# Softmax normalisation on ScalarE, head by head, in place of one VectorE product over four heads

## Chip, cores and metric

The kernel runs on one core of one Trainium2 chip. The metric is device time in microseconds; the kernel before takes 1180.76 us, the median of three runs (1177.13 to 1182.51). Engines are called by their names in the profile too: TensorE is PE (PEld its weight loads), VectorE DVE, ScalarE ACT, GpSimd POOL, and SyncE, which only issues DMAs here, SP.

## What is computed

One inference step of a two-layer decoder. Each layer normalises x (1024 prompt tokens and 8 sample tokens, 1024 channels), projects it through one matrix to pooling, attention and RWKV-7 inputs with their gates, and projects the concatenated results back. The change touches the attention, a sliding window of 128 with a learned sink per head:

```python
def _sink_softmax(s, mask, sinks):
    s = jnp.where(mask, s, -jnp.inf)
    sink = sinks.astype(jnp.float32)[:, :, None, None]
    m = jnp.maximum(jnp.max(s, axis=-1, keepdims=True), sink)
    p = jnp.exp(s - m)
    denom = jnp.sum(p, axis=-1, keepdims=True) + jnp.exp(sink - m)
    return p / denom

# per block of 128 queries:
p = _sink_softmax(s, mask, sinks.reshape(N_KV, Q_PER_KV))
o = jnp.einsum('bnkgqs,bnskd->bnqkgd', p.astype(vx.dtype), vx)
```

All values are float32. There are 8 heads of 64 channels, 2 key heads.

## The kernel before

**Stages.** The tokens are worked in two halves (H = 0: 512 prompt tokens and the 8 samples; H = 1: 512). Line 1542 and after give the order: input projection of layer 0 half 0, of half 1, output projection of half 0, then layer 1 half 0, output of layer 0 half 1, layer 1 half 1, and the two output projections of layer 1. Each projection multiplies high and low parts of weights and activations (three products per 128 channels, `acc<-hh,wh`, `acc<-hl,wh`, `acc<-hh,wl`, line 310). These products are "the projection products" below. The weights come by DMA, ScalarE casts their high part (`wh`) and GpSimd or VectorE makes the low part (`wl`).

**Streams beside the projections.** Attention, RWKV and the ends of the projection tiles are generators that run as jobs beside the projections (lines 270 to 352). Between two projection products `tick` lets every job go on whose due time has come. A due time is worked out by a planner: `Engine` (lines 120 to 152) books each VectorE, ScalarE and GpSimd instruction on that engine's account with a fixed part and a part per column (ScalarE 0.11 us and 0.00082 us a column, VectorE 0.07 and 0.00104, lines 162 to 164), and `after` (line 320) adds a margin to the time at which an operand should be there. TensorE's order is fixed by this planner; the order on the other engines is chosen by the framework's scheduler. Where a result is needed before anything else can go on, `need` (line 345) runs the jobs without projection products between them.

**Attention.** A block (`attn_block`, line 1135) is 128 queries of four heads: 2 layers times 2 halves times 4 query blocks times 2 groups of heads, 32 in all, and one sample job per layer (`attn_sample`). Its score products are `ps`. ScalarE and VectorE bring the current and the previous window into one tile `sm` of 128 queries by four heads by 129 columns, the sink in the last. `softmax` (line 1114) takes the minimum (the signs are turned), ScalarE's four exponentials with their sums, VectorE's reciprocal of the sums, and the product. Then `attn_values` (line 1173) transposes each head (`pt`), makes `pcur` (VectorE) and `pall` (ScalarE), and multiplies by the values (`po`). Three `sm` tiles exist, so a block's scores wait until the block three before is done; one block at a time may be between `pt` and `po` (`hold`, line 283). `open_attn` (line 1394) lets the next half's keys be finished only when all attention of the half before is done.

**RWKV.** Its scan goes in steps of 32 tokens, each with three small TensorE groups into `CA` and `CB`: from `XS,AG`, from `ys,TZ`, and from `XS,BT`, with short VectorE and ScalarE copies between. After eight steps come a group norm (`osb`, `gsm`) and the transposes back (`back`), then products on GpSimd. The last such group has to be done before line 1517, since the last products need it.

Of the kernel before, what the change touches and what calls it, by code (L numbers as in the profile page):

```python
# [12 lines left out]
AF = mybir.ActivationFunctionType  # L13
ALU = mybir.AluOpType
# [72 lines left out]
def hybrid_step_kernel(ctx: ExitStack, tc: tile.TileContext, I, O):  # L87
# [74 lines left out]
    V = Engine(nc.vector, 0.07, 0.00104)  # L162
# [93 lines left out]
    def tt(eng, out, a, b, op):  # L256
        eng.tensor_tensor(out=out, in0=a, in1=b, op=op)

    def act(out, in_, f, **kw):
        S.activation(out=out, in_=in_, func=f, **kw)  # L260
# [853 lines left out]
    def softmax(s, rows, nh):  # L1114

        sm = sb.tile([128, 2, 4], F32, tag="asm", name="asm", bufs=2)
        nm, su = (sm[:rows, i, :nh] for i in range(2))
        V.tensor_reduce(out=nm, in_=s, axis=AX.X, op=ALU.min)
        for i in range(nh):
            act(s[:, i, :], s[:, i, :], AF.Exp, scale=-1.0, bias=nm[:, i:i + 1], accum_out=su[:, i:i + 1])  # L1120
        V.reciprocal(out=su, in_=su)
        tt(V, s[:, :, 0:128], s[:, :, 0:128], su.unsqueeze(2).to_broadcast([rows, nh, 128]), ALU.mult)


    scored = []
# [9 lines left out]
    def attn_block(L, q, att, i, jp, mixed, after):  # L1135
# [25 lines left out]
        for e in range(2):  # L1161
# [4 lines left out]
            )  # L1166
        s4 = sm.rearrange("p e j k -> p (e j) k")
        softmax(s4, 128, 4)
        job = spawn(at_s[1], attn_values(L, att, i, jp, s4, done), (sm,))
        attn_jobs.append(job)  # L1170
# [34 lines left out]
    def attn_sample(L, q, att):  # L1205
# [30 lines left out]
        S.copy(out=s[:64, :128], in_=ps[:64, :128])  # L1236
        G.tensor_copy(out=s[:64, 128:129], in_=L.vd[:64, 17:18])
        softmax(s[:64].unsqueeze(1), 64, 1)
        yield (s,)
        yield from vacant("att")  # L1240
# [474 lines left out]
```

## Time and profile before

| | us |
|---|---|
| median of three runs | 1180.76 |
| the profiled execution, device time | 1182.06 |
| its span, first to last instruction | 1180.3 |
| PE busy | 1087.3 (92%) |
| DVE busy | 827.0 (70%) |
| ACT busy | 619.5 (52%) |
| POOL busy | 354.6 (30%) |
| mean granted TensorE clock | 0.958 of full |

How to read it: a busy TensorE is not TensorE at its peak, since matmuls are pipelined and their ends are modelled. Idle time of an engine that is not the bottleneck costs nothing. A group with one line (L150, L310) is recorded by a helper, so groups are told apart by the tile names; `sm<-sm,asm` is the softmax, `asm` the minimum and the sums.

### The profile page before, as it was taken

To read this page: it belongs to the slowest core of one execution; us is meant where nothing else is said; L and a number is where in the kernel's file an instruction comes from. 1 tells how busy PE (TensorE), PEld (TensorE's weight loads), DVE (VectorE), ACT (ScalarE), POOL (GpSimd) and SP (SyncE) were. 2 spreads that over 40 slices of the span, in tenths; PEclk is the share of its full clock that TensorE was granted. 3 is DMA by queue.
4 is the path that set the end of the run, shared out by engine and by line. 5 is a ranking of instruction groups with operands and counts; after the bars stand their busy time and mean duration, and the time that the engine had idled before them with its cause. 6 is when DMAs were issued, how large, how long until landed. Compare 5 with 4: busy or idle time off the path is not lost.

```text
span 1180.3 us, 24735 instructions
## 1 busy us (share of the span) xinstructions
PE 1087.3 (92%) x9258; PEld 872.2 (74%) x9258; DVE 827.0 (70%) x1783; ACT 619.5 (52%) x1579; POOL 354.6 (30%) x420
## 2 busy tenths in 40 slices
PE   6989897899899998989999979899999999899995
PEld 5989886576577677868988868666677677678864
DVE  6545889658867968577766988676855788877423
ACT  4435454557456663666446553475546566645331
POOL 5156535400131134430344534211112112333100
PEclk7999999999899998999999999899999999899997
DMA  6765344653255245644654335644575343454652
GB/s 194 225 195 167 120 142 152 201 182 102 77 170 153 75 143 170 211 152 138 197 166 126 111 106 152 223 139 157 194 227 171 119 153 107 132 184 145 184 155 93
DMA packets 116947, 183.27 MB, mean 155 GB/s; under 512 B 24398, under 2 KB 36190, under 8 KB 116828
## 3 DMA queue, kind: packets, MB, share of 16 engines
q1 hardware_dynamic: 116828, 181.70, 49.0%
q8 instruction: 72, 1.18, 0.4%
q14 instruction: 47, 0.39, 0.1%
HBM read 125.73 MB, written 50.62 MB: 149 GB/s over the span
## 4 chain that ended last, share of the span: by engine, by line
PE 61%; DVE 23%; DMA 4%; ACT 4%; issue 4%; POOL 2%; SPq 1%; POOLq 0%; DVEq 0%; ACTq 0%
PE acc L310 43%; PE CA L310 5%; DVE pr L150 3%; PE ps L310 2%; PE po L310 2%; PE CB L310 2%; DVE hl L150 2%; DMA sq<-z 2%; DVE sm L150 2%; DVE AG L150 1%; SPq L160 1%; DVE X L150 1%; PE pt L313 1%; DVE pd L150 1%; DVE z L150 1%
## 5 line engine op out<-in xcount | busy, mean ns | idle before, releaser
L310 PE MATMUL acc<-hh,wh 128*128 128x512 f32 (+2 forms) x1464 | 494.7, 338 | 17.9 <-ACT hh L150 9.4
L310 PE MATMUL acc<-hl,wh 128*128 128x256 f32 (+3 forms) x1464 | 493.8, 338 | 13.5 <-DVE hl L150 13.2
L310 PE MATMUL acc<-hh,wl 128*128 128x512 f32 (+2 forms) x1464 | 494.2, 339 | 8.7 <-POOL wl L150 5.7
L310 PEld LDWEIGHTS acc<-hh,wh 128*128 128x128 f32 x1464 | 284.8, 195 | 54.2 <-ACT hh L150 11.1
L310 PEld LDWEIGHTS acc<-hl,wh 128*128 128x128 f32 (+1 forms) x1464 | 282.9, 193 | 47.9 <-DVE hl L150 19.5
L310 PEld LDWEIGHTS acc<-hh,wl 128*128 128x128 f32 x1464 | 284.7, 195 | 45.2 <-issue 11.7
L150 ACT CAST wh<-wst 128x512 fp32r<-128x512 f32 (+1 forms) x246 | 148.8, 607 | 159.8 <-PE acc L310 109.8
L150 POOL TENSOR_TENSOR wl<-wst,wh 128x512 fp32r<-128x512 f32 x99 | 137.0, 1390 | 141.4 <-ACT wh L150 112.6
L150 DVE TENSOR_TENSOR pr<-X,N 128x4 f32<-128x4 f32 (+15 forms) x128 | 63.9, 499 | 6.8 <-POOL ro L150 3.2
L150 ACT ACTIVATE sm<-sm,asm 128x129 f32<-128x129 f32 x130 | 50.8, 393 | 17.5 <-DVE asm L150 17.3
L150 ACT ACTIVATE e<-e 128x520 f32<-128x520 f32 (+1 forms) x64 | 40.5, 633 | 26.7 <-DVE e L150 26.3
L150 POOL TENSOR_TENSOR z<-z,rope 128x520 f32<-128x520 f32 (+1 forms) x20 | 32.2, 1612 | 72.3 <-DMA sq<-z 59.9
L150 DVE TENSOR_REDUCE X<-pr 128x2 f32<-128x4 f32 (+15 forms) x128 | 44.8, 350 | 2.3
L150 POOL TENSOR_TENSOR mx<-mx,e 128x520 f32<-128x520 f32 (+1 forms) x24 | 33.2, 1381 | 42.5 <-ACT e L150 36.9
L150 ACT COPY XS<-CB 32x128 f32<-32x128 f32 (+2 forms) x88 | 27.3, 311 | 34.9 <-PE CB L310 34.2
L150 POOL TENSOR_TENSOR on<-on,bv 128x256 f32<-128x256 f32 x16 | 12.1, 779 | 110.5 <-ACT on L150 91.2
L150 ACT ACTIVATE XS<-CB,pc 64x64 f32<-64x64 f32 x112 | 28.7, 304 | 29.5 <-PE CB L310 28.4
L310 PE MATMUL ps<-kh,q 64*128 64x256 f32 (+1 forms) x256 | 39.0, 397 | 4.6 <-DVE sm L150 3.5
L150 POOL COPY sm<-vd 128x4 f32<-128x4 f32 (+1 forms) x34 | 8.2, 244 | 111.1 <-PE pt L313 81.8
L150 POOL COPY zs<-ev 128x9 f32<-128x9 f32 (+3 forms) x28 | 8.3, 298 | 107.1 <-DVE ev L150 90.2
L150 DVE COPY XS<-CA 32x128 f32<-32x128 f32 (+1 forms) x72 | 20.7, 288 | 26.8 <-PE CB L310 25.2
L150 DVE SCALAR_TENSOR_TENSOR hl<-xh,vec,hh 128x520 fp32r<-128x520 f32 (+1 forms) x32 | 28.0, 887 | 15.5 <-ACT hh L150 15.3
(250 smaller groups left out, 1925.5 us busy)
## 6 DMA issues: line engine op xcount, KB each, us to landing
wst<-in_w_in_dram SPq DMA_DIRECT2D x175, 256.0 KB, 3.1
kin<-wl SPq DMA_DIRECT2D x88, 256.0 KB, 3.4
wl<-kin SPq DMA_DIRECT2D x88, 256.0 KB, 2.7
wst<-in_w_out_dram SPq DMA_DIRECT2D x56, 256.0 KB, 3.5
kout<-wl SPq DMA_DIRECT2D x32, 256.0 KB, 3.5
zr<-mz SPq DMA_DIRECT2D x24, 256.0 KB, 3.2
xrkv<-zr SPq DMA_DIRECT2D x16, 384.0 KB, 4.1
wl<-kout SPq DMA_DIRECT2D x24, 256.0 KB, 3.1
```

Of the source, the lines that this page charges most:

```text
L150: return f(*a, **kw)
L160: return nc.sync.dma_start(out, in_)
L310: placed(T.matmul(out=out, lhsT=lhsT, rhs=rhs, start=start, stop=stop, **kw), n, out)
L313: placed(T.transpose(out=out, in_=in_, identity=identity), 300 if out.shape[0] > 64 else 130, out)
```

## The change

In `softmax` the one VectorE product of `sm` (128 queries by four heads by 128 columns) with the reciprocal sums, spread over the columns, is replaced by a loop over the heads: ScalarE copies each head's 128 columns in place, with the reciprocal sum of the row as a scale.

```diff
@@ -1119,7 +1119,8 @@
         for i in range(nh):
             act(s[:, i, :], s[:, i, :], AF.Exp, scale=-1.0, bias=nm[:, i:i + 1], accum_out=su[:, i:i + 1])
         V.reciprocal(out=su, in_=su)
-        tt(V, s[:, :, 0:128], s[:, :, 0:128], su.unsqueeze(2).to_broadcast([rows, nh, 128]), ALU.mult)
+        for i in range(nh):
+            act(s[:, i, 0:128], s[:, i, 0:128], AF.Copy, scale=su[:, i:i + 1])
 
 
     scored = []
```

The planner books the copies on ScalarE's account, so due times and with them the order of jobs shift. Three places follow; the orders before are given first.

ScalarE, layer 0 half 0, at the first three softmaxes (`sm,asm<-sm,asm` are the exponentials, `e`, `sq` and `XS` belong to gates, norms and RWKV). Before:

```order
L150 ACTIVATE sm,asm<-sm,asm 128x129 x4
L150 CAST wh_94<-wst 128x512
L150 ACTIVATE sm,asm<-sm,asm 128x129 x4
L150 COPY sm<-ps 128x2x128
L150 ACTIVATE sq<-xrkv,vec 128x256
L150 COPY sm<-ps 128x2x128
L150 CAST wh_95<-wst 128x512
L150 ACTIVATE e<-mx_665 128x520
L150 ACTIVATE e<-e 128x520
L150 ACTIVATE sm,asm<-sm,asm 128x129 x4
L150 ACTIVATE e<-e 128x520
```

After:

```order
L150 ACTIVATE sm,asm<-sm,asm 128x129 x4
L150 CAST wh_94<-wst 128x512
L150 ACTIVATE sm,asm<-sm,asm 128x129 x3
L150 CAST wh_95<-wst 128x512
L150 ACTIVATE sm,asm<-sm,asm 128x129
L150 ACTIVATE e<-mx_665 128x520
L150 ACTIVATE sq<-xrkv,vec 128x256
L150 ACTIVATE sm<-sm,asm 128x128 x4
L150 COPY sm<-ps 128x2x128 x2
L150 ACTIVATE sm<-sm,asm 128x128 x4
L150 ACTIVATE e<-e 128x520
```

The copies `sm<-sm,asm` 128x128 stand seven rows behind the first of their exponentials for the first softmax and seven for the second, with other work between, and the cast of `wh_95` moved ahead of the second softmax's last exponential.

TensorE at the end of the layer 1 half 1 RWKV, just before the last products. Before:

```order
L310 MATMUL acc<-hh,wh_93 128x512
L310 MATMUL acc<-hl,wh_93 128x512
L310 MATMUL acc<-hh,wl_96 128x512
L310 MATMUL CA<-XS,AG 32x64 x4
L310 MATMUL CB<-XS,AG 32x64 x4
L310 MATMUL CA<-ys,TZ 32x64 x2
L310 MATMUL CB<-ys,TZ 32x64 x2
L310 MATMUL CA<-XS,BT 64x64 x2
L310 MATMUL CB<-XS,BT 64x64 x2
L310 MATMUL CB<-XS,AG 32x64 x4
L310 MATMUL back<-cst,osb 64x64 x16
L310 MATMUL acc<-hh,wh_94 128x512
```

After:

```order
L310 MATMUL CB<-XS,AG 32x64 x4
L310 MATMUL acc<-hh,wh_95 128x512
L310 MATMUL acc<-hl,wh_95 128x512
L310 MATMUL acc<-hh,wl_98 128x512
L310 MATMUL acc<-hh,wh_93 128x512
L310 MATMUL acc<-hl,wh_93 128x512
L310 MATMUL acc<-hh,wl_96 128x512
L310 MATMUL acc<-hh,wh_93 128x512
L310 MATMUL acc<-hl,wh_93 128x512
L310 MATMUL acc<-hh,wl_96 128x512
L310 MATMUL back<-cst,osb 64x64 x16
L310 MATMUL acc<-hh,wh_94 128x512
```

Three groups of steps and the last one stood behind the last projection product before `back`; now the last step stands nine products ahead of `back`.

TensorE in layer 0, where the attention of half 0 has to end and no projection products are left (`ps<-kc` are the sample's scores, `xrkv` begins the next RWKV group). Before:

```order
L310 MATMUL ps<-kc,qp 64x128 x8
L313 MATMUL pt<-cst,sm 128x128 x4
L310 MATMUL CA<-XS,AG 32x64 x4
L310 MATMUL CB<-XS,AG 32x64 x4
L310 MATMUL CA<-ys,TZ 32x64 x2
L310 MATMUL CB<-ys,TZ 32x64 x2
L310 MATMUL po<-pall,vt 64x256
L310 MATMUL po<-pcur,vf 64x256
L310 MATMUL po<-pall,vt 64x256
L310 MATMUL po<-pcur,vf 64x256
L313 MATMUL pt<-cst,sm 128x128 x4
L310 MATMUL CA<-XS,BT 64x64 x2
```

After:

```order
L310 MATMUL ps<-kc,qp 64x128 x8
L313 MATMUL pt<-cst,sm 128x128 x4
L310 MATMUL CA<-ys,TZ 32x64 x2
L310 MATMUL CB<-ys,TZ 32x64 x2
L310 MATMUL CA<-XS,BT 64x64 x2
L310 MATMUL CB<-XS,BT 64x64 x2
L310 MATMUL po<-pcur,vf 64x256 x2
L313 MATMUL pt<-cst,sm 128x128 x4
L310 MATMUL CB<-XS,AG 32x64 x4
L310 MATMUL CA<-cst,xrkv 32x64 x16
L310 MATMUL CB<-cst,xrkv 32x64 x16
L310 MATMUL ps<-kh,q 128x256 x4
```

Between the last projection product before this place and the next one there were transposes of two blocks and of the sample; now there are those of four blocks and of the sample, and the first products of the next RWKV group, `CA` and `CB` from `xrkv` and from `BK`, and `back` stand in it too.

## Rows read from the trace of the kernel before

**Rows 1.** Part 1 of the page: busy us, share of the span, instructions.

```profile
PE 1087.3 (92%) x9258; PEld 872.2 (74%) x9258; DVE 827.0 (70%) x1783; ACT 619.5 (52%) x1579; POOL 354.6 (30%) x420
```

**Rows 2.** Part 4 of the page: the chain that ended last, by engine.

```profile
PE 61%; DVE 23%; DMA 4%; ACT 4%; issue 4%; POOL 2%; SPq 1%; POOLq 0%; DVEq 0%; ACTq 0%
```

**Rows 3.** Waits of TensorE: waiter, awaited, us in total, times, longest.

```profile
PE back L310 <- DVE osb L150: 9.3, 2, 4.7
...
PE ps L310 <- DVE sm L150: 3.5, 3, 2.0
...
PE po L310 <- DVE sm L150: 2.5, 3, 2.0
```

**Rows 4.** Groups by shape: names, shapes, count; busy us, mean ns; idle before.

```profile
L150 DVE TENSOR_TENSOR sm<-sm,asm 128x512 f32<-128x512 f32 x32 | 23.0, 718 | 0.6
...
L150 ACT ACTIVATE mz<-ev,vec 128x511 f32<-128x511 f32 x24 | 17.3, 721 | 2.0 <-DVE ev L150 1.3 <-POOL zs L150 0.3
...
L150 ACT ACTIVATE mz<-zs,vec 128x1 f32<-128x1 f32 x12 | 3.5, 288 | 0.0
```

**Rows 5.** Stretches: length, busy us (instructions) of PE, PEld, DVE, ACT, POOL; PEclk, DMA, GB/s.

```profile
180.00:200.00 20.00, 16.17 (x114) 14.27 (x114) 19.70 (x32) 7.66 (x16) 11.49 (x9) 1.00 0.53 159
...
260.00:280.00 20.00, 20.00 (x151) 13.83 (x152) 17.03 (x50) 15.52 (x49) 1.19 (x4) 1.00 0.29 96
...
300.00:320.00 20.00, 15.59 (x157) 11.06 (x158) 16.91 (x72) 6.32 (x24) 2.48 (x8) 0.83 0.17 60
...
960.00:980.00 20.00, 20.00 (x236) 14.89 (x235) 16.62 (x32) 16.23 (x50) 2.66 (x4) 1.00 0.41 127
```

**Rows 6.** Timeline, ScalarE then VectorE, 304 us: start, length, instruction, wait.

```profile
304.34 0.51 ACT L150 ACTIVATE XS<-CB,pc 64x64 f32<-64x64 f32 x2
...
304.93 0.16 DVE L150 RECIPROCAL asm<-asm 128x4 f32<-128x4 f32 x1
...
305.12 0.69 DVE L150 TENSOR_TENSOR sm<-sm,asm 128x512 f32<-128x512 f32 x1
```

**Rows 7.** Timeline, VectorE then TensorE, around 484 us.

```profile
483.03 0.69 DVE L150 TENSOR_TENSOR sm<-sm,asm 128x512 f32<-128x512 f32 x1
...
484.25 0.66 PE L313 MATMUL pt<-cst,sm 128*128 128x128 f32 x4
```

**Rows 8.** Timeline of TensorE: a step between products, and the tail.

```profile
1134.89 0.39 PE L310 MATMUL acc<-hh,wh 128*128 128x512 f32 x1
1135.12 0.40 PE L310 MATMUL acc<-hl,wh 128*128 128x512 f32 x1
...
1135.81 0.50 PE L310 MATMUL acc<-hh,wl 128*128 128x512 f32 x1
...
1149.92 0.40 PE L310 MATMUL acc<-hh,wl 128*128 128x512 f32 x1
...
1152.87 0.32 PE L310 MATMUL CB<-XS,AG 128*32 128x64 f32 x8 [0.39 <-ACT XS L150]
...
1163.37 0.80 PE L310 MATMUL acc<-hh,wh 128*128 128x512 f32 x1 [3.48 <-ACT hh L150]
```

**Rows 9.** Timeline of TensorE: drain of the first half's attention.

```profile
297.08 0.39 PE L310 MATMUL acc<-hh,wl 128*128 128x512 f32 x1
297.40 1.18 PE L310 MATMUL ps<-kh,q 64*128 64x256 f32 x8
...
308.33 1.11 PE L313 MATMUL pt<-cst,sm 128*128 128x128 f32 x4
...
311.88 0.66 PE L313 MATMUL pt<-cst,sm 128*128 128x128 f32 x4
...
318.93 0.80 PE L310 MATMUL acc<-hh,wh 128*128 128x512 f32 x1
```

**Rows 10.** Timeline, VectorE then TensorE, around 704 us.

```profile
703.55 0.68 DVE L150 TENSOR_TENSOR sm<-sm,asm 128x512 f32<-128x512 f32 x1
...
708.49 0.80 PE L310 MATMUL back<-cst,osb 64*64 64x64 f32 x10 [4.62 <-DVE osb L150]
```

## Prediction

> **What bounds the kernel now.** I read the page first. TensorE is busy for 92% of the span, VectorE for 70%, ScalarE for 52% [rows 1]. In the chain of waits that ended last, TensorE holds 61%, VectorE 23% and ScalarE 4% [rows 2]: the kernel runs at the pace of TensorE's instructions, and where TensorE has to wait it is mostly for VectorE. The list of TensorE's waits says for what [rows 3]: 9.3 us in two waits of `back` (the transposes behind the RWKV output's group norm) for `osb`, and 3.5 and 2.5 us in which attention's `ps` and `po` stood behind a VectorE step on `sm`; no wait for ScalarE within the attention is as long as these. So the change takes work from the second-busiest engine, which ends waits, and gives it to the third, which hardly does. The table by stretch of time shows the limit of that reading [rows 5]: where VectorE is full (19.70 of 20 us), TensorE falls to 16.17 of 20, and in two of the attention stretches ScalarE already stands at 15.52 and 16.23 of 20.
>
> **What is removed.** 32 products of 128x512 at 718 ns, 23.0 us of VectorE [rows 4], and two small ones in the two sample softmaxes. They sit right behind the reciprocal (304.93, then 305.12) [rows 6].
>
> **What is added.** Four ScalarE copies of 128x128 with a column as scale per softmax, 128 in all, and two small ones. No such copy of this size is in the trace. ScalarE's copy with a column as scale takes 288 ns for one column and 721 ns for 511 [rows 4], so 0.85 ns a column and 0.40 us for 128. The lower end is a pair of scaled copies of 64 columns that took 0.51 us together [rows 6]: 0.255 each, with 64 columns more 0.31, so 1.24 us for four, and the upper end is no overlap, 1.6 us. I take 1.3, since the pair is the same kind of instruction back to back. ScalarE gets 32 times 1.3 = 42 us, VectorE gives back 23. A softmax becomes 1.3 - 0.7 = 0.6 us longer, and the sum moves to an engine with more room. No function table has to be loaded for them, since copies with a column as scale run already (the `mz` groups [rows 4]).
>
> The latency alone costs nothing I can find. The smallest distances between the end of the product and the next transpose group are 0.53 us (483.03 + 0.69 to 484.25 [rows 7]) and a near equal one at 1061 us; the others have more than 1 us. Taken at 0 to +1; I take 0. What is late next in these two places is the transpose itself, by 0.1 us.
>
> [...]
>
> **What is moved.** The planner counts the four copies on its ScalarE account (0.86 us by its constants, less than the 1.3 above) and drops the product from VectorE's, so every later due time shifts, and with it TensorE's order from the first attention value step on. I compared the two orders place by place and priced the differences with rows.
>
> (a) *Tail.* Before the last products, the last RWKV group must be finished. In the order before, its last steps (AG, ys, BT, AG) stand with no projection products between them. From the last product (1149.92) to the next (1163.37) 13.45 us pass, and the last step is issued at 1152.87 [rows 8]. In the changed order the last step stands nine products ahead of `back`. A product follows the one before after 0.23 us, with a step between them after 0.69 [rows 8]. So the hole becomes 1163.37 - 1152.87 = 10.5 less 9 times 0.23 = 8.4 us, which is 5.0 less; three steps then lie among products, at 0.69 - 0.23 = 0.46 each, 1.4. **Gain 3.6**; bounds 2 and 5 (a step that waits; no cost for the steps).
>
> (b) *Drain of the first half's attention* (layer 0). All attention of one half must end before the next half's keys are finished, and here the projection products run out: 297.08 to 318.93, 21.9 us without them [rows 9]. Two blocks' transposes are in it before, four after. One block later costs 311.88 - 308.33 = 3.55 us [rows 9], together +7. But the changed order also puts other TensorE work into this hole that stood among products before (four groups of 32 small products, `back`, two `ps` groups, and two blocks' `pt` and `po`): about 10 us of issue, so the hole is longer and fuller. Against that, the last block's scores come late: from `ps` (297.40 [rows 9]) to the end of the product (305.8 [rows 6]) 8.4 us pass, with 0.6 more after. **Cost 1**; bounds -3 and +9.
>
> (c) *Sample attention of layer 1.* It ends later, at the point where the next half's keys need it, with a step pair uncovered; the price of such a pair is the like of 0.5 us in (a), and a rope table behind it. **Cost 1**; bounds 0 and 3.
>
> (d) *The other wait of `back`* (708.49, 4.62 us [rows 10]). VectorE's queue held `osb` up; a softmax product stood in it at 703.55, and the one before that too. Both go, 1.4 us, and the surroundings are less dense after. **Gain 2**; bounds 0 and 4.6.
>
> (e) *VectorE elsewhere in attention.* The 6.0 us of `ps` and `po` behind `sm` [rows 3] contain at most one product each. **Gain 2**; bounds 0 and 6.
>
> (f) *ScalarE's queue.* It runs in order, and the copies stand in front of weight casts (`wh`), which TensorE needs. In 960 to 980 us three softmaxes would bring 16.23 to 20.1 of 20 [rows 5], while the new order spreads them somewhat. **Cost 2**; bounds 0 and 9.
>
> Sum: -3.6 + 1 + 1 - 2 - 2 + 2 = -3.6. The profiled execution took 1182.1 us (span 1180.3 and 1.8 around it), 1.3 above the median of the runs. So 1178.5 for that one and 1177.2 for the median.
>
> **Rivals.**
> *VectorE's relief counts in full* (faster): the gains of (a), (d) and (e) at their upper ends, 5 + 4.6 + 6 = 15.6, with the costs of (b), (c) and (f) as taken, 4, and a further 2 lost in new waits: -10, **1171**. For it: VectorE's 23% of the chain. Against it: TensorE's own work comes right behind, and a new order finds new waits.
>
> *ScalarE becomes the bound in the attention stretches* (slower): the point from which it decides is a stretch in which it is busy for over 19 of 20 us. TensorE is busy for 18.4 us of 20 on average (92% [rows 1]) and was for 16.2 beside a full VectorE [rows 5], 2.2 less; in the six stretches of 20 us with the most softmaxes (260 to 300, 380 to 400, 760 to 800, 960 to 980) that is 13 us in place of the 2 in (f): **1188**. For it: 15.5 and 16.2 now, and a planner that counts the copies too short. Against it: no wait of weight for ScalarE today.
>
> *The drain grows* (slower): (b) at +9, with TensorE at its lower clock behind the longer hole for some 2 us more: **1187**. From 300 to 320 us the granted clock is 0.83 of full already now, after the waits of the drain [rows 5].
>
> *Every softmax on the path* (slower): the transposes follow the copies at once wherever the new order puts them, and all 32 softmaxes pass their 0.6 us on, 19 us, **1196**. Against it: the distance in [rows 7] is among the two smallest of all. [...]
>
> That the change doesn't do what it says is no rival: the order holds all 130 copies and no product.
>
> **How the numbers follow.** Forecast 1177.2 (own range 1173 to 1184): 0.41. Full relief 0.31, ScalarE bound 0.17, drain 0.08, every softmax 0.03. The range from 1166 to 1190 leaves out the last rival and what lies beyond the others. About 0.5%, 5.9 us, is what a measurement of this kernel can tell from no change: faster is under 1174.9, slower over 1186.7. Full relief and a little of the forecast's lower end give 0.34 faster; the three slower rivals 0.28 slower; 0.38 the same.
>
> **What would show it.** After: VectorE busy near 804 us, ScalarE near 655 to 660; each copy 0.36 to 0.42 us; at the tail one wait of `back` and one for `hh` with no `ys` or `XS` wait ahead, and the last hole near 8.5 us; no 4.6 us wait of `back` in layer 1's first half. The forecast is wrong if ScalarE shows 19 of 20 us in a stretch with TensorE under 17, or the first drain over 32 us.

## The result, and the profile after

The changed kernel takes 1198.2 us against 1180.8 (1177.1 to 1182.5), a ratio of 1.0136, 95% interval 1.0109 to 1.0164. The 1198.2 is the median of three runs, 1196.8, 1198.2 and a slow one of 2469.5, which the ratio leaves out. It is slower by 17 us, where the forecast was 1177.2 and the range ended at 1190.

The engines did what was expected of them. Part 1 of the page of the changed kernel, then the group of the copies by shape (columns as in [rows 1] and [rows 4]):

```profile
PE 1092.5 (91%) x9258; PEld 877.8 (73%) x9258; DVE 802.4 (67%) x1749; ACT 657.7 (55%) x1709; POOL 346.8 (29%) x420
```

```profile
L150 ACT ACTIVATE sm<-sm,asm 128x128 f32<-128x128 f32 x128 | 41.3, 393 | 6.7 <-DVE asm L150 6.4
```

In the timeline of ScalarE four of them stand back to back and take 1.28 us together (start, duration):

```profile
291.25 1.28 ACT L150 ACTIVATE sm<-sm,asm 128x128 f32<-128x128 f32 x4
```

VectorE gave back 24.6 us and ScalarE took 38.2. TensorE's busy time rose by 5.2 us for the same 9258 instructions, and the span by 14.7, so 9.5 us of the loss are idle time and 5.2 are the same instructions taking longer.

The chain of waits by engine [rows 2] has TensorE at 56% where it was 61, and TensorE's waits are spread otherwise (total, times, longest; the columns of [rows 3]):

```profile
PE 56%; DVE 22%; DMA 7%; ACT 6%; issue 4%; POOL 3%; SPq 2%; POOLq 0%; DVEq 0%; ACTq 0%
```

```profile
PE acc L310 <- ACT hh L150: 15.0, 6, 3.8
PE acc L310 <- DVE hl L150: 7.9, 12, 1.5
PE CA L310 <- DVE XS L150: 6.8, 6, 3.4
...
PE po L310 <- DVE sm L150: 5.1, 3, 2.8
PE CA L310 <- DVE TZ L150: 4.7, 2, 4.2
...
PE back L310 <- DVE osb L150: 3.5, 1, 3.5
...
PE acc L310 <- ACT wh L150: 1.7, 2, 1.1
PE ps L310 <- DVE sm L150: 1.6, 3, 0.9
```

In the kernel before, the two longest were:

```profile
PE acc L310 <- DVE hl L150: 19.4, 16, 3.0
PE acc L310 <- ACT hh L150: 10.1, 5, 3.8
```

The waits for `hl` and of `back` for `osb` shrank; those for `hh`, `XS`, `TZ` and of `po` for `sm` grew.

To find the place, I set the times at which VectorE reads each finished accumulator (their order is fixed by the program) side by side. The changed kernel is 2.7 us ahead at 299 us (times of the kernel before) and 18.3 behind at 334; 31.7 behind at 523; 32.6 at 639; 4.3 at 829; 27 at 1026; 19.9 at 1145 and 14.7 at the end. By far the steepest piece is the first: 21 us within 35. It is the drain of layer 0's first half, of which [rows 9] show the kernel before. The same place in the changed kernel, TensorE's rows (start, duration, then the instruction and in brackets its wait):

```profile
293.33 0.40 PE L310 MATMUL acc<-hh,wl 128*128 128x512 f32 x1
...
297.55 0.44 PE L310 MATMUL CA<-XS,AG 128*32 128x64 f32 x8 [3.44 <-DVE XS L150]
...
308.98 1.30 PE L310 MATMUL ps<-kc,qp 128*64 128x128 f32 x5 [2.65 <-DVE ys L150]
...
324.08 0.66 PE L310 MATMUL po<-pall,vt 128*64 128x256 f32 x4 [2.78 <-DVE sm L150]
...
335.90 0.79 PE L310 MATMUL acc<-hh,wh 128*128 128x512 f32 x1
340.92 0.42 PE L310 MATMUL CA<-ys,TZ 128*32 128x64 f32 x2 [4.22 <-DVE TZ L150]
...
343.42 0.78 PE L310 MATMUL acc<-hl,wh 128*128 128x512 f32 x1
```

From the last projection product to the next one 42.6 us pass (293.33 to 335.90), where it was 21.9. Here is the whole place in both kernels, from that last product to the reading of the same next accumulator (stretch and its length; busy time of TensorE, its weight loads, VectorE, ScalarE, GpSimd; granted clock, DMA share, GB/s). First before, then after:

```profile
297.08:333.83 36.75, 31.29 (x380) 23.51 (x379) 32.65 (x95) 15.15 (x43) 7.10 (x13) 0.91 0.37 113
```

```profile
293.33:352.13 58.80, 42.50 (x430) 30.43 (x429) 40.81 (x116) 28.69 (x87) 9.31 (x19) 0.80 0.21 66
```

It is 22.0 us longer: TensorE's idle time grows from 5.5 to 16.3, by 10.8, and its busy time by 11.2. Fifty more instructions account for a part of the second and the lower clock, a mean of 0.80 in place of 0.91, for the rest. An estimate from these two rows: busy time times granted clock is 28.5 before and 34.0 after, so some 5.5 us are more work and some 5.7 the lower clock. The 22 us are thus about half waits, a quarter work that stood elsewhere before, and a quarter slower work. The hole without products alone, first before and then after:

```profile
297.08:318.93 21.85, 16.39 (x173) 11.69 (x172) 18.80 (x68) 7.57 (x28) 3.49 (x11) 0.84 0.23 74
```

```profile
293.33:335.90 42.57, 31.04 (x362) 22.20 (x361) 29.00 (x88) 23.01 (x74) 6.20 (x17) 0.80 0.18 57
```

Of the 10.8 us of idle time 6.1 lie in the hole (5.5 before, 11.5 after) and the rest behind it, nearly all in the wait for `TZ`. Over the whole stretch VectorE isn't full here (40.8 of 58.8 us) and ScalarE still less so. By stretches of 20 us, as in [rows 5]:

```profile
280.00:300.00 20.00, 16.57 (x194) 11.88 (x186) 15.78 (x38) 14.17 (x44) 3.01 (x8) 0.94 0.25 83
300.00:320.00 20.00, 14.97 (x169) 10.80 (x167) 12.97 (x48) 10.66 (x39) 1.29 (x4) 0.72 0.16 54
320.00:340.00 20.00, 13.63 (x162) 9.65 (x162) 13.73 (x40) 11.46 (x32) 3.37 (x7) 0.88 0.21 67
340.00:360.00 20.00, 18.55 (x113) 13.94 (x113) 12.02 (x25) 9.37 (x22) 4.39 (x3) 0.87 0.34 101
```

The tail, on the other hand, came out as forecast. TensorE's last products in the changed kernel, to be read beside [rows 8]:

```profile
1169.70 0.40 PE L310 MATMUL acc<-hh,wl 128*128 128x512 f32 x1
1173.58 1.15 PE L310 MATMUL back<-cst,osb 64*64 64x64 f32 x32 [3.48 <-DVE osb L150]
1178.21 0.79 PE L310 MATMUL acc<-hh,wh 128*128 128x512 f32 x1 [3.48 <-ACT hh L150]
```

The hole is 8.5 us (forecast 8.4, before 13.45), with one wait of `back` and one for `hh`.

### The profile page after: what moved, and what is told of

Read it like the earlier page. It is cut to its first block, busy times and chain, and to the rows that moved or that the text cites. A ratio compares the mean times of both kernels' runs of the same rounds, so it can differ in the third digit from the quotient of the medians.

```text
span 1195.0 us, 24779 instructions
## 1 busy us (share of the span) xinstructions
PE 1092.5 (91%) x9258; PEld 877.8 (73%) x9258; DVE 802.4 (67%) x1749; ACT 657.7 (55%) x1709; POOL 346.8 (29%) x420
## 3 DMA queue, kind: packets, MB, share of 16 engines
q8 instruction: 72, 1.18, 0.4%
## 4 chain that ended last, share of the span: by engine, by line
PE 56%; DVE 22%; DMA 7%; ACT 6%; issue 4%; POOL 3%; SPq 2%; POOLq 0%; DVEq 0%; ACTq 0%
PE acc L310 40%; PE CA L310 5%; DVE pr L150 3%; PE ps L310 2%; PE po L310 2%; SPq L160 2%; DVE AG L150 2%; DVE X L150 2%; ACT sm L150 2%; PE CB L310 2%; DMA xh<-in_x_dram 1%; DMA sq<-z 1%; DVE hl L150 1%; DMA wst<-in_w_in_dram 1%; DVE N L150 1%
## 5 line engine op out<-in xcount | busy, mean ns | idle before, releaser
L150 ACT ACTIVATE sm<-sm,asm 128x128 f32<-128x128 f32 (+3 forms) x260 | 92.8, 392 | 33.8 <-DVE asm L150 33.3
L310 PEld LDWEIGHTS CA<-ys,TZ 128*32 128x32 f32 x256 | 16.4, 111 | 25.7 <-issue 9.6
```

The lines of the kernel that those rows point to most:

```text
L150: return f(*a, **kw)
L310: placed(T.matmul(out=out, lhsT=lhsT, rhs=rhs, start=start, stop=stop, **kw), n, out)
```

## Experiments

The change does two things at once: it moves work between engines, and it changes what the planner books, so that TensorE's order is another one. The first four runs part the two. In them `only_booked(V)` enters an instruction in the planner's accounts without issuing it, and `nc.scalar` or `nc.vector` issues one without booking it. Each diff shows the lines that matter, without the helper `only_booked`, against the changed kernel unless the text names another. Ratios are to the kernel before on the same chip.

### Work without the order, and the order without the work

**e1.** Copies on ScalarE, booked as the old product (TensorE's order of before):

```diff
-        for i in range(nh):
-            act(s[:, i, 0:128], s[:, i, 0:128], AF.Copy, scale=su[:, i:i + 1])
+        tt(only_booked(V), s[:, :, 0:128], s[:, :, 0:128], su.unsqueeze(2).to_broadcast([rows, nh, 128]), ALU.mult)
+        for i in range(nh):
+            nc.scalar.activation(out=s[:, i, 0:128], in_=s[:, i, 0:128], func=AF.Copy, scale=su[:, i:i + 1])
```

> The four scaled copies run on ScalarE as in the changed kernel, but the planner books what it booked before (one product on VectorE), so TensorE's order is that of the kernel before, instruction for instruction. Theory A (the loss comes from the re-planned order, not from the copies): no slower than before, 1172 to 1183 us, with VectorE near 804 and ScalarE near 656 us busy, and the first drain from the last product (297.1 us in the kernel before) to the next no longer than its 21.9 us by more than 2 us. Theory B (the copies themselves cost: their 0.6 us more per softmax, and ScalarE's queue): 1192 to 1200 us, as the changed kernel.

Measured: 1170.6 us, ratio 0.9898 (0.9874 to 0.9921). VectorE 802.2, ScalarE 654.0, drain 19.5 us (296.71 to 316.17). Theory A holds (the time is even 1.4 us under its range), and this version beats both kernels.

**e2.** The product on VectorE, booked as four copies (TensorE's order of after):

```diff
+        for i in range(nh):
+            only_booked(S).activation(out=s[:, i, 0:128], in_=s[:, i, 0:128], func=AF.Copy, scale=su[:, i:i + 1])
+        nc.vector.tensor_tensor(
+            out=s[:, :, 0:128], in0=s[:, :, 0:128], in1=su.unsqueeze(2).to_broadcast([rows, nh, 128]), op=ALU.mult
+        )
```

> The converse: the product runs on VectorE as before, but the planner books four ScalarE copies, so TensorE's order is that of the changed kernel, instruction for instruction. Theory A (order): 1192 to 1206 us, with the long drain (42.6 us without projection products in the changed kernel) again over 38 us. Theory B (copies): 1176 to 1186 us, drain under 30 us.

Measured: 1205.7 us, ratio 1.0191 (1.0168 to 1.0214), drain 42.5 us (291.95 to 334.42). Again theory A. The four corners fit together: the new order costs 24 us with the product and 28 with the copies, and the copies give 11 us in the old order and 7 to 8 in the new. The work moved the way it was meant to; the order that came with it cost more than twice that.

Where does the old order gain? The same stretch of layer 1's first half, by the same two accumulators, in the kernel before and in the run with copies in its order:

```profile
649.40:757.64 108.24, 93.88 (x820) 79.82 (x820) 91.92 (x187) 51.63 (x133) 47.29 (x49) 0.91 0.43 133
```

```profile
644.40:745.14 100.74, 88.53 (x821) 75.44 (x820) 91.08 (x185) 55.52 (x145) 44.37 (x49) 0.98 0.45 144
```

7.5 us less: 2.1 of them idle time and 5.4 busy time, at a clock of 0.98 in place of 0.91. The wait of `back` for `osb` [rows 10] falls from 4.6 to 3.1 us here. Fewer waits and a higher granted clock go together in this stretch.

### Is it the drain, or the whole order?

**e3.** The nine softmaxes of layer 0's first half booked as before, the others as in the changed kernel:

```diff
+        calls[0] += 1
+        if calls[0] <= 9:
+            tt(only_booked(V), s[:, :, 0:128], s[:, :, 0:128], su.unsqueeze(2).to_broadcast([rows, nh, 128]), ALU.mult)
+        else:
+            for i in range(nh):
+                only_booked(S).activation(out=s[:, i, 0:128], in_=s[:, i, 0:128], func=AF.Copy, scale=su[:, i:i + 1])
```

> All copies on ScalarE; the planner books the nine softmaxes of layer 0's first half as before and the rest as in the changed kernel. TensorE's order is that of the kernel before up to product 1949 of 5934, behind the drain, and a new one from there. Theory A1 (the drain's order is the loss, the rest is even): the drain is back at 20 to 24 us and the time is the changed kernel's less about 21, 1172 to 1181 us. Theory A2 (any re-planned order scatters, and the drain was only its largest piece here): the drain is back, but the time lies anywhere from 1172 to 1196 us.

Measured: 1182.1 us, ratio 1.0003 (0.9983 to 1.0022). The drain is back at 19.4 us, but of the 27.6 us between the changed kernel and e1 only 16.1 are back; 11.5 come out of an order that is new only from product 1949 on. The time is one microsecond above A1's 1181, too little to decide between the theories; that this order and e1's differ by 11.5 us, with equal drains, is what speaks for A2.

**e4.** The converse (`calls[0] > 9`):

> The converse of the run before: the nine softmaxes of layer 0's first half are booked as in the changed kernel, the rest as before; TensorE's order is the changed kernel's up to product 1927 of 5934, which takes in its long drain. Theory A1 (the drain is the loss): about 21 us over the kernel before less what VectorE's relief gives, 1194 to 1204 us. Theory A2 (scatter of the whole order): the drain is long again, over 38 us, but the time lies anywhere from 1180 to 1204 us. Theory B has nothing to say on the drain here, and gives the changed kernel's 1197 us.

Measured: 1195.5 us, ratio 1.0094 (1.0061 to 1.0127), drain 42.8 us. Both theories allow it. Together the two runs say that the drain is the largest piece of the loss and not the only one.

### What holds the drain up

In the changed kernel's drain the inverse of the next RWKV group (`pr`, `X`) stands still for 15 us. VectorE's rows there:

```profile
308.12 0.36 DVE L150 TENSOR_REDUCE X<-pr 128x10 f32<-128x200 f32 x1
...
322.00 0.69 DVE L150 TENSOR_REDUCE gsm<-gsq 128x8 f32<-128x512 f32 x1 [2.71 <-ACT gsq L150]
323.58 0.45 DVE L150 COPY_PREDICATED sm<-cst,ps 128x256 f32<-128x256 int32 x1 [0.90 <-ACT sm L150]
323.91 0.43 DVE L150 TENSOR_TENSOR pr<-X,N 128x264 f32<-128x264 f32 x1
...
335.58 0.57 DVE L150 TENSOR_TENSOR pr<-X,N 128x392 f32<-128x392 f32 x1 [1.53 <-POOL ro L150]
...
340.43 1.82 DVE L150 STREAM_TRANSPOSE TZ<-X 32x256 f32<-32x256 f32 x4
```

`gsq` and `on` of the group norm share the one buffer of `pr`, and both were in it when the inverse wanted it. **e5.** So they were moved to a tile that is dead by then:

```diff
-        sq = sb.tile([128, 8, 64], F32, tag="pr", name="gsq")
+        dead = AG.rearrange("p c a e x t -> p (c a e x t)")
+        sq = dead[:, 0:512].rearrange("p (c v) -> p c v", c=8)
...
-        on2 = sb.tile([128, 2, 256], F32, tag="pr", name="on")
+        on2 = dead[:, 512:1024].rearrange("p (a v) -> p a v", a=2)
```

> The changed kernel, TensorE's order untouched, but the squares of the RWKV group norm and its output (`gsq`, `on`) no longer use the one buffer of `pr`, in which the next group's inverse (`pr`, `X`) forms its products; they lie in the dead `AG` of their own group. In the changed kernel's drain the inverse makes no step from 308.1 to 323.9 us and from 328.7 to 335.6, in both cases with a `gsq` or `on` in that buffer, and TensorE's last wait of the stretch (4.2 us at 340.92) is for the `TZ` that comes out of it. Theory P (the shared buffer delays the inverse, and this is part of the loss): that wait goes, with 0 to 4 us more where VectorE's queue stood behind a step of the inverse; 1187 to 1194 us. Theory N (the waits of the drain come from too little work beside the attention's serial steps): the inverse comes early and nothing else moves, another wait takes its place; 1194 to 1200 us.

Measured: 1190.1 us, ratio 1.0070 (1.0041 to 1.0098), against 1.0136 for the changed kernel. VectorE, then TensorE at the end of the drain:

```profile
316.34 0.69 DVE L150 TENSOR_REDUCE X<-pr 128x16 f32<-128x512 f32 x1
...
318.23 1.77 DVE L150 STREAM_TRANSPOSE TZ<-X 32x256 f32<-32x256 f32 x4
```

```profile
336.97 0.80 PE L310 MATMUL acc<-hh,wh 128*128 128x512 f32 x1
337.70 0.24 PE L310 MATMUL CA<-ys,TZ 128*32 128x64 f32 x1
```

`TZ` is there 22 us earlier (318.23 for 340.43), and the wait of 4.2 us is gone. Theory P holds, but the hole ahead of that wait is as long as ever (293.13 to 336.97, 43.8 us). In the two traces, by the same accumulators as above, this kernel is 0.2 us ahead of the changed one before the drain, 3.8 behind it, 9.3 at 639 us and 11.0 at the end, so most of what it gains arises later, and no run shows where from. By its rows, what fills the hole is the chain of blocks that had to end there, one `ps`, softmax, `pt` and `po` after the other, with no projection products beside them; no run tests that by itself.

**e6.** The same two tiles moved in e1's kernel:

> The same two tiles moved, in the kernel that copies on ScalarE with TensorE's order of the kernel before (e1_act_booked_dve, 1170.6 us). In the drain of that order the last step of the inverse also stands behind the group norm (327.12 us), but TensorE has 33 us of projection products beside it. Theory P: 0 to 4 us less than that run, 1166 to 1171 us, from places other than the drain. Theory N: no difference, 1169 to 1173 us.

Measured: 1171.3 us, ratio 0.9888 (0.9851 to 0.9926), beside 0.9898: no difference that the intervals could show. Theory N, in that order, though P's 1171 lies only 0.3 us off.

### Which part of the booking?

The changed kernel books four pieces in a chain, so a softmax is due 0.79 us later, and on another account. **e7** changes the account alone (the copies are issued unbooked, as in e1):

```diff
+        at = at_of(s, su) + M2
+        end = place(S.busy, at, V.fixed + V.per * 128 * nh)
+        there(s, end + 0.0)
```

> Copies on ScalarE, booked on ScalarE's account as one piece of the product's old cost, 0.60 us, so a softmax's due time is as before and only the account differs (the changed kernel books four pieces in a chain, each 0.178 us after the one before: 1.57 us against 0.78). At the point where the first half's attention must end, 45 groups of TensorE's instructions stand without products (37 before, 50 in the changed kernel). Theory D (the later due time alone pushes blocks into the drain): close to e1_act_booked_dve, 1168 to 1178 us. Theory A2 (every change of a booking gives another order, and the time scatters with it): anywhere from 1170 to 1206 us, with a drain over 26 us.

Measured: 1193.7 us, ratio 1.0084 (1.0058 to 1.0110), drain 32.5 us.

**e8** changes the due time alone, again with unbooked copies:

```diff
+        at = at_of(s, su) + M2
+        end = place(V.busy, at, V.fixed + V.per * 128 * nh)
+        there(s, end + 0.79)
```

> Copies on ScalarE, booked on VectorE's account with the product's cost as before, but due 0.79 us later, which is what the chained booking adds. 41 groups stand without products at the end of the first half's attention. Theory D (due time): as the changed kernel, 1190 to 1202 us, with a drain over 38 us. Theory A2 (scatter): anywhere from 1170 to 1206 us, the drain by the count between those of before (21.9) and after (42.6).

Measured: 1194.5 us, ratio 1.0087 (1.0056 to 1.0117), drain 23.0 us. Theory D falls on e7 by time and drain, and on e8 by the drain, though e8's time is in its range: the run with the old due time is slow with a long drain, and the one with the late due time is slow with a short one. A2 is left.

### How far does the time scatter with the order?

**e9 to e11.** e1's kernel (old booking, 1170.6 us) with one constant of the planner changed each time that is not the softmax's own, the first of these three in e9, the second in e10, the third in e11. The constants hold for the softmax too, as for every VectorE instruction, every instruction and every attention step, but each is changed by only 0.002 to 0.02 us.

```diff
-    V = Engine(nc.vector, 0.07, 0.00104)
+    V = Engine(nc.vector, 0.072, 0.00104)
...
-M2 = 0.178
+M2 = 0.18
...
-MA0 = 1.98
+MA0 = 2.0
```

> e1_act_booked_dve (copies on ScalarE, booked as the product was; 1170.6 us) with one constant of the planner changed that has nothing to do with this change: a fixed 0.072 us per VectorE instruction in its accounts in place of 0.07. The order differs from product 606 on, and only 17 groups of TensorE's instructions stand without products at the end of the first half's attention (37 in the order of before). Theory S (the order of before is a lucky or selected one, and nearly every other order of the same planner is slower): 1178 to 1200 us, though this drain is shorter than any so far. Theory L (the loss came from what this change books, so unrelated small changes do little): 1164 to 1176 us.

Measured: 1186.7 us, ratio 1.0018 (0.9990 to 1.0046).

> The same kernel as the run before, with another unrelated constant: the planner's margin from an input to an instruction, 0.18 us in place of 0.178. The order differs from product 606 on; 43 groups in the drain. Theory S: 1178 to 1200 us. Theory L: 1166 to 1178 us.

Measured: 1201.8 us, ratio 1.0164 (1.0121 to 1.0206), drain 32.8 us.

> The same kernel again, with a third constant: the least margin of the attention streams, 2.0 us in place of 1.98. The order differs from product 816 on; 37 groups in the drain, as before. Theory S: 1176 to 1198 us, from places other than the drain. Theory L: 1166 to 1176 us.

Measured: 1173.1 us, ratio 0.9915 (0.9889 to 0.9942), drain 19.4 us. Two against theory L (e10 lies even above the range of S), one for it: one to three hundredths of a constant move the time by 16, 31 and 2.5 us, the largest as much as the new order of the change did and the smallest within the noise.

**e14 to e16.** The changed kernel with the same three constants.

> The changed kernel, with the unrelated constant of e9_constant_v (0.072 for 0.07 us per VectorE instruction). 28 groups stand without products at the end of layer 0's first half and 35 at that of layer 1's. Theory O (the order scatters, whatever moves it): anywhere from 1173 to 1204 us, and the mean of the three runs of this kind within 6 us of the 1187.2 that the same constants gave with the old booking. Theory K (the chained booking is bad by itself): slower than e9's 1186.7 by over 5 us, and a mean of the three over 1194.

Measured: 1182.3 us, ratio 1.0000 (0.9974 to 1.0025), drain 23.1 us, with a second one of 21.3 us in layer 1 (901.01 to 922.34).

> The changed kernel, with the unrelated constant of e10_constant_m2 (margin 0.18 for 0.178). 57 groups stand in the first drain, the most of all. Theory O: anywhere from 1173 to 1206 us. Theory K: slower than e10's 1201.8 us.

Measured: 1191.3 us, ratio 1.0069 (1.0043 to 1.0094), drain 51.5 us.

> The changed kernel, with the unrelated constant of e11_constant_ma0 (2.0 for 1.98). 50 groups in the first drain, as in the changed kernel itself. Theory O: anywhere from 1173 to 1204 us. Theory K: 1190 us or more, against e11's 1173.1.

Measured: 1203.6 us, ratio 1.0178 (1.0124 to 1.0231), drain 43.1 us. With the second constant the changed booking is the faster one by 10 us, with the third the slower by 30, and with the first the intervals overlap; the means are 1192.4 and 1187.2: theory O, by less than its 6 us, while K holds on e16 alone. That the chained booking is bad by itself isn't shown.

All orders with copies on ScalarE, by the length of the first drain (last product to next, each from its own trace; the order of e9 breaks its drain up with products between, and its longest piece there is 7.2):

| order | drain, us | time, us |
|---|---|---|
| old, e1 | 19.5 | 1170.6 |
| new: e9, e3, e11, e8, e14 | 7.2, 19.4, 19.4, 23.0, 23.1 | 1186.7, 1182.1, 1173.1, 1194.5, 1182.3 |
| new: e7, e10, after, e4, e16, e15 | 32.5, 32.8, 42.6, 42.8, 43.1, 51.5 | 1193.7, 1201.8, 1198.2, 1195.5, 1203.6, 1191.3 |

Eleven new orders have a mean of 1191 us and a standard deviation of 9; those with a short drain have a mean of 1184, those with a long one 1197. The old order is below all eleven, though e11 (0.9915) is not clear of it (0.9898). The count of TensorE's groups without products, as the expectations give it, goes with the drain in the main: 17, 28, 37, 41, 43, 45, 50 and 57 groups (e9, e14, e11, e8, e10, e7, after, e15) gave 7.2, 23.1, 19.4, 23.0, 32.8, 32.5, 42.6 and 51.5 us. With the time it goes only loosely: e8 and e15 take 1194.5 and 1191.3 us. Why the old order is the fastest is not shown; that the planner's constants, given to three digits, were chosen with this very order in view is only argued.

### What the copies cost when the order stands still

**e12.** Each copy followed by a second one with scale 1, in e1's kernel:

```diff
+        for i in range(nh):
+            nc.scalar.activation(out=s[:, i, 0:128], in_=s[:, i, 0:128], func=AF.Copy, scale=1.0)
```

> e1_act_booked_dve (1170.6 us) with each of the 130 copies followed by a second one of the same tile with scale 1, not booked, so that TensorE's order is unchanged: some 42 us more of ScalarE, 1.3 us more per softmax. Theory R (ScalarE has room and the softmax's latency is covered): 1169 to 1176 us. Theory Q (the copies stand in ScalarE's queue before what TensorE waits for, or the transposes follow them at once): 1182 us or more, up to 1170.6 + 42.

Measured: 1180.2 us, ratio 0.9985 (0.9958 to 1.0011), between R and Q. The added copies cost less than expected; ScalarE grew by 24.3 us (654.0 to 678.3), not 42, so 0.8 us per softmax and not 1.3. The copies by line, in that run (count, then shortest, median and longest in ns):

```profile
L1135 ACT ACTIVATE sm<-sm,asm x130: 384/392/424, 173.1 to 1092.8; 128x128 f32<-128x128 f32 x128, 64x128 f32<-64x128 f32 x2
L1137 ACT ACTIVATE sm<-sm x130: 292/302/322, 176.5 to 1094.2; 128x128 f32<-128x128 f32 x128, 64x128 f32<-64x128 f32 x2
```

**e13.** No normalisation at all, in the same order (the edit is against e1's kernel):

```diff
         tt(only_booked(V), s[:, :, 0:128], s[:, :, 0:128], su.unsqueeze(2).to_broadcast([rows, nh, 128]), ALU.mult)
-        for i in range(nh):
-            nc.scalar.activation(out=s[:, i, 0:128], in_=s[:, i, 0:128], func=AF.Copy, scale=su[:, i:i + 1])
```

> TensorE's order of the kernel before, and the softmax is not normalised at all (neither product nor copies; the part that is left out). Beside e1_act_booked_dve (1170.6 us, copies once) and e12_copies_twice (1180.2) it gives the price of the copies, and beside the kernel before (1182) that of VectorE's product. Theory Lin (each softmax's 1.3 us of copies costs the same wherever it is added): 1158 to 1164 us. Theory Cov (the first 1.3 us are covered, only more than that reaches TensorE): 1167 to 1173 us.

Measured: 1174.0 us, ratio 0.9920 (0.9891 to 0.9948). Theory Cov, a microsecond above its range: without copies the kernel is no faster than with them (0.9898), so the first 1.3 us per softmax are covered in this order, and only a second helping (e12) makes the kernel slower, by 10 us. The product on VectorE, by the same run, cost the kernel before 9 us (11 by e1).

## Why the prediction was wrong

*The price of the copies* was right: 0.39 us each (estimated 0.40), four in 1.28 us (1.3). Nor was a table load added: each of the two traces holds one, of 1.28 us, 0.7 us after the start. VectorE at 802 and ScalarE at 658 were where they were expected (804, 655 to 660).

*Latency, taken at 0*: right in the old order, where leaving the copies out gained nothing (e13).

*(a) Tail, gain 3.6*: right for the hole, which went from 13.45 to 8.5 us, 4.9 less (5.0 expected); from the last product before it to the end of the span it is 5.1 less. The 1.4 us set against it, for three steps among products, no run isolates.

*(b) Drain, cost 1, bounds -3 and +9*: this is the step that failed. It cost 21 us from 299 to 334 us, and 16.1 came back when only the order up to behind the drain was put back (e3). The term had +7 for the two more blocks, and set against it the work moved into the hole, some 10 us that made it "fuller", and the late scores; no row gave that balance of 1. The moved work stands between the blocks in TensorE's fixed order, and the blocks' steps wait for each other all the same: idle time went up by 10.8 us, 6.1 in the hole and 4.7 behind it, in the wait for `TZ`, which is in no term. And I allowed 2 us for the clock, in a rival, where it took some 5.7. The rival of the growing drain had the right place and mechanism at a chance of 0.08, with half the price. The prediction's own sign of being wrong, a first drain over 32 us, is the one that came.

*(c) Sample attention of layer 1, cost 1*: not isolated by any run.

*(d) The wait of `back` at 708, gain 2*: the wait is gone in the changed kernel. In the old order it is 0.7 us without product and copies (e13), 3.1 with the copies (e1) and 5.3 with the copies twice (e12): VectorE's relief takes nearly all of it, and the copies on ScalarE, which the term did not count, give a good part back (one trace each).

*(e) VectorE elsewhere, gain 2*: no gain in the waits named. `ps` and `po` behind `sm` took 3.5 and 2.5 us before [rows 3], and 1.6 and 5.1 after. In the old order (e1) they took 2.3 and 2.0, while `pt` behind `sm` grew from 0.4 to 1.8.

*(f) ScalarE's queue, cost 2*: no more than that by the weight casts (`wh`), which delay TensorE for 1.7 us in all. The waits for `hh`, which ScalarE makes too, grew from 10.1 to 15.0 us, but are 8.7 with the same copies in the old order (e1), so the new order brought that. ScalarE did run in order where the lists of the program and the trace can be laid side by side (170 to 177 us of the changed kernel). And the fullest of the 60 stretches of 20 us (160 to 180) has ScalarE busy for 16.5. The rival *ScalarE becomes the bound* is out.

*VectorE's relief in full* (1171) is the time of the run with the old order, though 5 us of its sum are (a), which belongs to the new order. *Every softmax on the path* (1196) comes within 2.2 us of the result and is wrong: with the copies in the old order the kernel is faster, so it was the right time by the wrong mechanism: luck. In the engines' busy time the trade is a loss, 38 us more of ScalarE for 25 less of VectorE in the changed kernel and 34.5 for 24.8 in e1, but not in the kernel's: e1 measured 0.9898.

Behind (b) is the larger error. The sum treated a new order as the old one with a few local differences, each with a row's price. But places that I didn't look at moved the changed kernel by +13 (334 to 523 us), -28 (639 to 829) and +23 (829 to 1026), some of it work that only changed its place. E3, with the drain repaired, is still 11.5 us over the old order, and the eleven new orders scatter with 9 us. A sum of row prices doesn't reach that; a range of 24 us about 1177 was centred on an order that no longer existed.

## What to carry over

When a change alters what a planner books, ask first what a new order alone costs: perturb an unrelated constant a few times and take that spread and mean as a term of the sum. Then harvest the work without the order, by booking what was booked before: here that turned a change of +1.4% into one of -1.0%. And look at the points at which a serial chain must end before the next products may start; what the new order left undone there was the largest piece of the loss here.

## What was not expected of the hardware

In the drain, waits came with slower work around them, at a lower granted clock, which the list of waits does not show: 10.8 us more of idle time came with a clock of 0.80 for 0.91, worth some 5.7 us more of busy time by the estimate above. One instruction group shows it: eight `ps` products took 1.18 us at 297.40 in the kernel before [rows 9], and in the changed kernel, behind the wait of 3.44 us, they took 2.08:

```profile
298.13 2.08 PE L310 MATMUL ps<-kh,q 64*128 64x256 f32 x8
```

The granted clock of these two stretches, before and after (last column but two), is 1.00 and 0.50 of full:

```profile
297.40:298.58 1.18, 1.18 (x13) 0.85 (x16) 1.18 (x1) 0.64 (x3) 0.00 (x0) 1.00 0.18 16
```

```profile
298.13:300.21 2.08, 2.08 (x12) 1.19 (x8) 1.43 (x6) 0.21 (x1) 0.31 (x3) 0.50 0.00 0
```

The two fell together as well: in a stretch of layer 1's first half (649.40 to 757.64 before, 644.40 to 745.14 in e1, 820 and 821 instructions of TensorE) e1 has 2.1 us of idle time less and 5.4 us of busy time less, at 0.98 for 0.91.

But equal idle time came with unequal clocks here. In the hole of the old order TensorE idles for 5.46 us in the kernel before and for 5.45 in e1, whose row is:

```profile
296.71:316.17 19.46, 14.01 (x174) 9.79 (x172) 18.17 (x68) 10.16 (x37) 2.82 (x11) 1.00 0.27 83
```

The clock is 0.84 in the one and 1.00 in the other, and the hole is 2.4 us shorter, all of it busy time (16.39 us before, 14.01 in e1, for 173 and 174 instructions). The copies are not the reason: e6, with e1's order and copies, has 0.84 and 21.6 us. What decides it, no run shows.
